# Equal-length matmuls in a row, and a model clock that holds traced matmul durations

## The chip, the core and the metric

The kernel runs on one core of a Trainium2 chip. The metric is the device time of one execution in microseconds; of the kernel before there are three runs. Engines are called by the profile's names: PE multiplies matrices, PEld is its weight loading, DVE, ACT and POOL are the vector, scalar and general engines, SP issues DMAs.

## The reference

Two layers act on one sequence of 256 tokens with 1024 features, all in float32. A layer is a feed-forward block, a mixer and a second feed-forward block:

```python
x = x + 0.5 * swiglu_ffn(rms_norm(x, ffn1_norm[l]), ffn1_w_gate_up[l], ffn1_w_down[l])
h = rms_norm(x, mix_norm[l])
rg_x, rg_g, sb_q, sb_k, sb_v, c_q, c_kv, k_r, gate_logits = jnp.split(h @ w_in[l], split_points, axis=-1)
...
merged = g_a * (y_a @ w_branch_a[l]) + g_b * (y_b @ w_branch_b[l]) + g_c * (y_c @ w_branch_c[l])
x = x + merged @ w_out[l]
x = x + 0.5 * swiglu_ffn(rms_norm(x, ffn2_norm[l]), ffn2_w_gate_up[l], ffn2_w_down[l])
```

The feed-forward blocks are 1024 to 2 x 2816 and 2816 to 1024. The mixer has three branches: a gated linear recurrence (`y_a`), an attention with stick-breaking weights over 8 heads (`y_b`), and an attention with low-rank queries and keys (`y_c`). A final normalisation ends it.

## The kernel before, in words

Activations are kept with the features on the partitions and the 256 tokens along the row. Every float32 value that enters a large product is split into a high part in the type float32r and the rest, also in float32r, and a product is made of three of the four part products: high by high, high by low, low by high.

The weights stream from HBM in units of 1 MB (the tile `raw`). A piece of 128 x 1024 of a unit is split by one copy on ACT (tile `hi`) and one subtraction on DVE (tile `lo`); three `raw`, four `hi` and four `lo` buffers rotate. The split activations lie in the tiles `r`, where the high and the low part of the same 128 features stand beside each other, 256 columns each.

Most products are made by `feature_group` (line 511). A group makes 2 x 128 output features for 256 tokens in two PSUM banks (tile `acc`, or two tiles `side`); the index `b` is the bank. For each 128 input features (one entry of `kts`) and each bank it issues two matmuls: one with the high weights as stationary operand and 512 moving columns, the activations' high and low part side by side (a hi matmul), and one with the low weights and only the 256 columns of the high part (a lo matmul), which adds to the first half of the same bank. `held` holds one entry of `kts` at a time, so one round of the loop is four matmuls. Only the closing entries of a group with `last` are collected to four. `token_group` and `narrow_group` make other layouts with matmuls of one length: 512, 256 or 320 columns.

A feed-forward block runs 22 groups of 8 entries for gate and up, and four groups of 22 entries for down (the last block has two token groups in their place). A mixer runs some 60 groups in the order of the table `MIX_ORDER` (line 31). Between them stands the side work: attention scores, cumulative sums, the recurrence's gates, transposes, normalisations. These are Python generators whose instructions are queued and put between the groups' matmuls by a planner (`Tasks`, line 222). After each round of a group `tick` looks at the front of every queue, and `fits` (line 266) asks a model clock whether the instruction may go: a side matmul goes if its inputs are ready at most 60 ns after the model's PE time, within a budget `SIDE` of 350 ns a round; an instruction on ACT or DVE goes if it starts soon after the model's PE time, and if it is not urgent it must also end within `LIMIT`, 1800 ns of it. `drain` puts in a task without asking, when a group needs its result. The model clock adds up costs per engine; the cost of an instruction is set in `Op.__init__` (line 180 for PE), and `emit` (line 195) also puts in an ACT table load where an activation needs a function that the loaded table does not hold. All engines run their instructions in the order in which they were put in.

All of this goes through one helper, so most rows of the profile bear line 201.

Of the kernel before, what the change touches and what calls it, by code (L numbers as in the profile page):

```python
# [6 lines left out]
F32 = mybir.dt.float32  # L7
F32R = mybir.dt.float32r
# [85 lines left out]
class Slots:  # L94


    def __init__(self, tiles):
        self.free = deque(tiles)
# [61 lines left out]
class Op:  # L160


    def __init__(self, engine, name, op, args, kw):
        self.f, self.e, self.args, self.kw = getattr(engine, op), name, args, kw
        self.engine = engine
        out = kw.get("out", args[0] if args else None)
        n = 1
        for d in out.shape[1:]:
            n *= d
        outs = [out] + ([kw["accum_out"]] if kw.get("accum_out") is not None else [])  # L170
        aps = [x for x in (*args, *kw.values()) if hasattr(x, "tensor")]
        self.outs = {x.tensor.name for x in outs}
        self.ins = {x.tensor.name for x in aps if all(x is not o for o in outs)}
        self.table, self.tail = None, 80
        if op == "dma_start":
            self.cost, self.tail = 50, 2500
        elif name == "pe":
            self.tail = 165
            wide = op == "matmul" and args[2].dtype == F32
            self.cost = 2.5 + 0.4167 * (4 * n if wide else max(n, 256))  # L180
        elif name == "act":
            self.table = TABLES.get(kw.get("func"))
            extra = sum(90 for k in ("scale", "bias") if not isinstance(kw.get(k, 0.0), (int, float)))
            self.cost = 95 + extra + 0.833 * n
        elif name == "dve":
            fast = op in ("tensor_scalar", "tensor_copy") and all(x.space != bass.MemoryType.PSUM for x in aps)
            rate = {"reciprocal": 6.5, "tensor_tensor_scan": 2.1}.get(op, 0.55 if fast else 1.042)
            self.cost = 68 + rate * n
        else:
            self.cost = 150 + (166 if kw.get("op") == ALU.pow else 2.1) * n  # L190

    def when(self, c, after=0.0):
        return c.start(self.e, self.ins, self.outs, after)
# [144 lines left out]
def trunk(tc, xT_in, pos_in, w_in, rgw_in, fin_in, const_in, out):  # L338
# [4 lines left out]
    with ctx:  # L343
# [86 lines left out]
        def next_sub():  # L430
            i = st["sub"]
            st["sub"] += 1
            split_to(i // 2 + AHEAD)
            h, lo = piece_t[i // 2]
            piece_t.pop(i // 2 - 1, None)
            c = slice((i % 2) * 512, (i % 2 + 1) * 512)
            return h[:, c], lo[:, c]
# [44 lines left out]
        def bank():  # L482
            while not acc.free:
                tasks.drain(pend[0], done=lambda: acc.free)
                if pend[0]["done"]:
                    pend.popleft()
            return acc.now()

        def small_banks():
            tasks.wait(lambda: len(side.free) >= NT)  # L490
            return [side.now() for _ in range(NT)]

        def finish(evac, a, early=None):
            t = tasks.spawn(evac(a), urgent=True, early=early)
            if type(a) is not list:
                pend.append(t)
            return t

        def bank_of(a, b):
            return a[b] if type(a) is list else a[:, b]  # L500
# [10 lines left out]
        def feature_group(kts, evac, last=0):  # L511


            nk = len(kts)
            a = small_banks() if last or nk <= 2 else bank()
            held = []
            for i, (h, _, hl) in enumerate(kts):
                if i % 2 == 0:
                    wh, wl = next_sub()
                held.append((i, h, hl, wh, wl))  # L520
                if nk - last <= i < nk - 1:
                    continue
                for b in range(2):
                    for j, h, hl, vh, vl in held:
                        c = slice((j % 2) * 256 + b * 128, (j % 2) * 256 + (b + 1) * 128)
                        pe.matmul(bank_of(a, b), vh[:, c], hl, start=j == 0, stop=False, skip_group_check=True)
                        pe.matmul(bank_of(a, b)[:, 0:256], vl[:, c], h, start=False, stop=j == nk - 1, skip_group_check=True)
                held = []
                tasks.tick()
            return finish(evac, a, tasks.LAST if last else None)  # L530
# [223 lines left out]
        def ffn(nm, ntasks, nxt, final=False, extra=None, xg=None):  # L754
# [24 lines left out]
            for c in range(KF):  # L779
                if xg and c < PLAIN:  # L780
                    ht[c] = plain_group(c, xg, gen_h(c), (ntasks, nm))
                    if c == 0:
                        split_to(2 * PLAIN + 1, 0)
                    if c == PLAIN - 1:
                        FT.give(*xg)
                else:
                    ht[c] = feature_group(kts, gen_h(c))
                if c == 6 and extra:
                    tasks.spawn(extra())
                if c == 3 and final:  # L790
                    xk = {}
                    tokens = tasks.spawn(tokens_of_x(xk))
# [16 lines left out]
            for n in () if final else range(4):  # L809
                out_tasks.append(feature_group(Hidden(), lambda a, n=n: update_x(n, a, 0.5, nxt), last=4 if n == 3 else 0))  # L810
                if n == 0:
                    FT.give(nm["rb tile"])
# [541 lines left out]
        for p in range(4):  # L1354
            for h in range(2 if p == 0 else 1):
                c = slice(h * 256, (h + 1) * 256) if p == 0 else slice(0, 512)
# [160 lines left out]
```

## Time and profile before

| | us |
|---|---|
| median of three runs (lowest, highest) | 1463.38 (1461.54, 1464.88) |
| the profiled execution's own time | 1464.41 |
| its span, first to last instruction | 1462.6 |
| PE busy | 1446.7 (99%) |
| DVE busy | 1110.9 (76%) |
| ACT busy | 889.7 (61%) |
| granted clock of PE, mean | 0.999 |

A matmul's row gives its start and how long it was in the pipeline; matmuls overlap there, so the time that one costs is read from the distance between starts, or from the number of matmuls in a window, and not from its own duration.

### The profile page before, as it was taken

The page shows a single profiled execution, that of the slowest core. Times are in us where ns is not written, and L with a number is a line of the kernel's source. Part 1 is how long each engine was busy: PE and PEld are TensorE (multiplying, and loading weights), DVE is VectorE, ACT ScalarE, POOL GpSimd, SP SyncE. Part 2 cuts the span into 40 slices and gives each one's busy share as a digit, 9 for nine tenths or more (in the row PEclk, how much of TensorE's full clock was granted, in tenths as well). Part 3 has the DMA queues.
Part 4 walks back from the last instruction along what each step waited for, and adds up shares of the span by engine and source line. Part 5 has one row for each costly group of instructions (what it writes and reads, how often), then busy time and mean ns, then how long its engine had stood idle before and what let it go on. Part 6 is the DMA issues. An engine that isn't in the chain of part 4 may idle for free.

```text
span 1462.6 us, 20835 instructions
## 1 busy us (share of the span) xinstructions
PE 1446.7 (99%) x8276; PEld 1264.1 (86%) x8276; DVE 1110.9 (76%) x1548; ACT 889.7 (61%) x1365; POOL 142.5 (10%) x118
## 2 busy tenths in 40 slices
PE   9999999999999999999999999999999999999998
PEld 8888889888888888888888888898888888888886
DVE  6887567689987788876677776676989877877853
ACT  4665446888665556565455554478885656566643
POOL 2000001123410000000000000111324000100001
PEclk9999999999999999999999999999999999999999
DMA  7554554444543455455545455544445434555552
GB/s 264 180 201 179 197 180 167 165 151 147 198 145 145 171 182 195 178 197 190 188 175 195 177 197 178 196 166 147 149 166 180 173 123 170 198 187 199 178 200 87
DMA packets 37507, 258.17 MB, mean 177 GB/s; under 512 B 4257, under 2 KB 4641, under 8 KB 6817
## 3 DMA queue, kind: packets, MB, share of 16 engines
q1 hardware_dynamic: 35856, 253.16, 48.0%
q0 software_dynamic: 832, 2.62, 0.6%
q8 instruction: 65, 1.06, 0.3%
q10 hardware_dynamic: 720, 1.05, 0.2%
q14 instruction: 34, 0.27, 0.1%
HBM read 255.77 MB, written 1.05 MB: 176 GB/s over the span
## 4 chain that ended last, share of the span: by engine, by line
PE 91%; DVE 6%; issue 1%; DMA 1%; ACT 1%; POOL 0%; ACTq 0%; POOLq 0%; DVEq 0%
PE acc L201 76%; PE side L201 15%; DVE lo L201 3%; DVE f L201 2%; DVE r L201 1%; DMA raw<-w 1%; ACT hi L201 0%; DMA x<-xT 0%; ACT f L201 0%; POOL rms L201 0%; ACT r L201 0%; ACTq L396 0%; POOLq L1513 0%; DVE rms L201 0%; DVEq L201 0%
## 5 line engine op out<-in xcount | busy, mean ns | idle before, releaser
L201 PE MATMUL acc<-r,hi 128*128 128x512 f32 x3116 | 1121.4, 402 | 0.0
L201 PE MATMUL acc<-r,lo 128*128 128x256 f32 x3116 | 871.5, 280 | 0.0
L201 DVE TENSOR_TENSOR lo<-raw,hi 128x1024 fp32r<-128x1024 f32 (+1 forms) x478 | 591.2, 1239 | 236.2 <-ACT hi L201 235.1
L201 PEld LDWEIGHTS acc<-r,hi 128*128 128x128 f32 x3116 | 584.9, 188 | 131.4
L201 PEld LDWEIGHTS acc<-r,lo 128*128 128x128 f32 x3116 | 588.1, 189 | 2.5
L201 ACT CAST hi<-raw 128x1024 fp32r<-128x1024 f32 (+1 forms) x478 | 497.0, 1045 | 134.8 <-PE acc L201 94.7
L201 POOL TENSOR_TENSOR f<-f,f 128x512 f32<-128x512 f32 (+1 forms) x51 | 89.5, 1761 | 1047.7 <-ACT f L201 963.9
L201 ACT COPY f<-acc 128x512 f32<-128x512 f32 x164 | 96.2, 586 | 124.3 <-PE acc L201 120.4
L201 ACT ACTIVATE f<-f 128x256 f32<-128x256 f32 (+3 forms) x190 | 94.9, 502 | 84.6 <-DVE f L201 83.4
L201 DVE TENSOR_TENSOR f<-acc,f 128x512 f32<-128x512 f32 x166 | 113.8, 686 | 39.9 <-ACT f L201 39.3
L201 DVE TENSOR_TENSOR f<-f,f 128x512 f32<-128x512 f32 (+1 forms) x177 | 125.0, 706 | 7.9 <-ACT f L201 1.6
L201 PE MATMUL acc<-hi,r 128*128 128x512 f32 (+2 forms) x344 | 96.8, 358 | 0.0
L201 ACT CAST r<-f 128x256 fp32r<-128x256 f32 (+2 forms) x130 | 58.5, 455 | 60.8 <-DVE f L201 59.8
L201 PE MATMUL side<-r,hi 128*128 128x512 f32 x260 | 92.3, 396 | 0.0
L201 PE MATMUL side<-r,lo 128*128 128x256 f32 x260 | 72.7, 280 | 0.0
L201 PE MATMUL side<-f,f 128*128 128x256 f32 (+1 forms) x320 | 71.5, 327 | 0.0
L201 PEld LDWEIGHTS acc<-hi,r 128*128 128x128 f32 x344 | 61.6, 189 | 8.4
L201 DVE TENSOR_TENSOR r<-f,r 128x256 fp32r<-128x256 f32 (+2 forms) x130 | 64.7, 502 | 1.9 <-ACT r L201 1.9
L201 PE MATMUL acc<-lo,r 128*128 128x512 f32 (+2 forms) x172 | 61.1, 355 | 0.0
L201 PEld LDWEIGHTS side<-r,hi 128*128 128x128 f32 x260 | 48.8, 188 | 11.3
L201 PEld LDWEIGHTS side<-f,f 128*128 128x128 f32 x320 | 45.8, 190 | 4.8
L201 PEld LDWEIGHTS side<-r,lo 128*128 128x128 f32 x260 | 49.0, 189 | 0.0
(95 smaller groups left out, 841.4 us busy)
## 6 DMA issues: line engine op xcount, KB each, us to landing
raw<-w SPq DMA_DIRECT2D x239, 1024.0 KB, 4.8
f<-rgw POOLq DMA_DIRECT2D x8, 256.0 KB, 3.3
raw<-w SPq DMA_DIRECT2D x4, 256.0 KB, 5.4
out<-f SPq DMA_DIRECT2D x4, 256.0 KB, 2.2
x<-xT ACTq DMA_DIRECT2D x3, 256.0 KB, 5.8
f<-fin POOLq DMA_DIRECT2D x2, 256.0 KB, 3.7
cst<-const SPq DMA_DIRECT2D x1, 336.0 KB, 7.7
x<-xT ACTq DMA_DIRECT2D x2, 128.0 KB, 4.0
```

Of the source, the lines that this page charges most:

```text
L201: return self.f(*self.args, **self.kw)
```

## The change

The loop of `feature_group` now issues the hi matmuls of both banks first and then the lo matmuls of both banks. Where `last` is set, each bank is still finished by itself, its hi matmuls first and then its lo matmuls. The model cost of a matmul on PE is given by a new function; the lengths, types and number of matmuls do not change.

```diff
             self.tail = 165
-            wide = op == "matmul" and args[2].dtype == F32
-            self.cost = 2.5 + 0.4167 * (4 * n if wide else max(n, 256))
+            self.cost = self.streamed(op, args[2].dtype if op == "matmul" else F32, n)
...
+    @staticmethod
+    def streamed(op, dtype, n):
+
+        if op == "transpose":
+            return max(109, 0.852 * n)
+        if dtype == F32:
+            return 2 * max(112, 0.852 * n)
+        if dtype == F32R:
+            return 13.5 + 0.4167 * max(n, 256)
+        return 30 + 0.4167 * n
...
-                for b in range(2):
-                    for j, h, hl, vh, vl in held:
-                        c = slice((j % 2) * 256 + b * 128, (j % 2) * 256 + (b + 1) * 128)
+                for bs in ((0,), (1,)) if last else ((0, 1),):
+                    work = [(b, j, h, hl, vh, vl, slice((j % 2) * 256 + b * 128, (j % 2) * 256 + (b + 1) * 128)) for b in bs for j, h, hl, vh, vl in held]
+                    for b, j, h, hl, vh, vl, c in work:
                         pe.matmul(bank_of(a, b), vh[:, c], hl, start=j == 0, stop=False, skip_group_check=True)
+                    for b, j, h, hl, vh, vl, c in work:
                         pe.matmul(bank_of(a, b)[:, 0:256], vl[:, c], h, start=False, stop=j == nk - 1, skip_group_check=True)
```

For a hi matmul of 512 columns the model cost goes from 215.9 to 226.9 ns, for a lo matmul of 256 columns from 109.2 to 120.2 ns.

The first place is PE in the gate and up groups of the first feed-forward block, three entries of `kts`; `acc_84` is a group's pair of banks, `r_90` and `r_91` are split activations. Before:

```order
L201 MATMUL acc_84<-r_90,hi 128x512
L201 MATMUL acc_84<-r_90,lo 128x256
L201 MATMUL acc_84<-r_90,hi 128x512
L201 MATMUL acc_84<-r_90,lo 128x256
L201 MATMUL acc_84<-r_90,hi 128x512
L201 MATMUL acc_84<-r_90,lo 128x256
L201 MATMUL acc_84<-r_90,hi 128x512
L201 MATMUL acc_84<-r_90,lo 128x256
L201 MATMUL acc_84<-r_91,hi 128x512
L201 MATMUL acc_84<-r_91,lo 128x256
L201 MATMUL acc_84<-r_91,hi 128x512
L201 MATMUL acc_84<-r_91,lo 128x256
```

The same twelve matmuls now:

```order
L211 MATMUL acc_84<-r_90,hi 128x512 x2
L211 MATMUL acc_84<-r_90,lo 128x256 x2
L211 MATMUL acc_84<-r_90,hi 128x512 x2
L211 MATMUL acc_84<-r_90,lo 128x256 x2
L211 MATMUL acc_84<-r_91,hi 128x512 x2
L211 MATMUL acc_84<-r_91,lo 128x256 x2
```

The lengths change every two matmuls and no longer at every one. In the seven groups with `last` (the last down group of three feed-forward blocks, and two groups of each mixer) the entries before the closing four keep the order of before, since one entry and one bank make a single hi and a single lo matmul; the closing four entries make runs of four.

The second place is ACT in the first layer's mixer, in the groups `rgg1` and `rgg2`; `f_112<-f_112 128x384` before and `f_136<-f_136 128x384` now is stick-breaking work, `f_118<-side_88,cst` now is a gate of the recurrence, `f_113` and `f_109` are gates. Before, twelve rows hold one table load:

```order
L136 ACT_TABLE_LOAD
L201 ACTIVATE f_109<-f_109 128x512
L201 CAST hi<-raw 128x1024
L201 ACTIVATE f_113<-f_110 128x512
L201 CAST hi<-raw 128x1024
L201 COPY f_123<-acc_84 128x512
L201 ACTIVATE f_141<-side_87 128x384
L201 CAST r_103<-f_121 128x512
L201 ACTIVATE f_112<-side_89 128x384
L201 ACTIVATE f_113<-f_113 128x512
L201 CAST hi<-raw 128x1024
L201 ACTIVATE f_136<-f_123 128x512
```

Now, a little earlier in the same mixer, three stand in twelve rows:

```order
L136 ACT_TABLE_LOAD
L211 ACTIVATE f_118<-side_88,cst 128x256
L211 ACTIVATE f_119<-side_88,cst 128x256
L211 ACTIVATE f_136<-side_86 128x384
L136 ACT_TABLE_LOAD
L211 ACTIVATE f_136<-f_136 128x384
L211 CAST hi<-raw 128x1024
L211 COPY f_137<-acc_84 128x512
L211 ACTIVATE f_136<-f_136 128x384
L136 ACT_TABLE_LOAD
L211 ACTIVATE f_121<-f_118,tiny,s_77 128x256
L211 CAST hi<-raw 128x1024
```

Recurrence and stick-breaking work now alternate on ACT, and each change of function loads a table. Over the whole kernel the order holds 33 table loads before and 45 now, the twelve more in the two mixers.

The third place is PE where the recurrence's last gates are computed, in the first layer's mixer; `side_86<-r_98,r_97` are those gates' products. Before, they stand in the groups `rgg3` and `gb0`:

```order
L201 MATMUL side_87<-f_112,f_119 128x128
L201 MATMUL side_86<-r_98,r_97 128x256 x2
L201 MATMUL acc_85<-r_92,hi 128x512
L201 MATMUL acc_85<-r_92,lo 128x256
L201 MATMUL acc_85<-r_92,hi 128x512
L201 MATMUL acc_85<-r_92,lo 128x256
L201 MATMUL side_86<-r_98,r_97 128x256 x4
L201 MATMUL acc_85<-r_92,hi 128x512
L201 MATMUL acc_85<-r_92,lo 128x256
L201 MATMUL acc_85<-r_92,hi 128x512
L201 MATMUL acc_85<-r_92,lo 128x256
L201 MATMUL side_88<-r_93,r_103 128x256 x4
```

Now the last of them stand some twenty matmul rounds later, in the group `gb2`:

```order
L211 MATMUL side_86<-r_93,r_104 128x256 x2
L211 MATMUL acc_84<-r_105,hi 128x512 x2
L211 MATMUL acc_84<-r_105,lo 128x256 x2
L211 MATMUL side_86<-r_93,r_104 128x256 x3
L211 MATMUL acc_84<-r_90,hi 128x512 x2
L211 MATMUL acc_84<-r_90,lo 128x256 x2
L211 MATMUL side_86<-r_93,r_104 128x256
```

Two pairs of the recurrence were fed together before (`r_98` and `r_93` in turn); now one pair is fed at a time, with rounds of the group between its matmuls.

## Rows read from the trace of the kernel before

**Rows 1.** The page: its first line, and part 1, engines.

```profile
span 1462.6 us, 20835 instructions
PE 1446.7 (99%) x8276; PEld 1264.1 (86%) x8276; DVE 1110.9 (76%) x1548; ACT 889.7 (61%) x1365; POOL 142.5 (10%) x118
```

**Rows 2.** Waits of PE: who waits for whom, us in total, times, longest.

```profile
PE side L201 <- DVE r L201: 4.7, 4, 1.5
PE side L201 <- DVE f L201: 2.0, 2, 1.1
```

**Rows 3.** Groups by form, whole span: count | busy us, mean ns | idle before.

```profile
L201 PE MATMUL acc<-r,hi 128*128 128x512 f32 x3116 | 1121.4, 402 | 0.0
...
L201 PE MATMUL side<-r,hi 128*128 128x512 f32 x260 | 92.3, 396 | 0.0
```

**Rows 4.** The same view, 30 to 190 us (first layer, first feed-forward block).

```profile
L201 PE MATMUL acc<-r,hi 128*128 128x512 f32 x433 | 153.0, 399 | 0.0
...
L201 PE MATMUL side<-r,hi 128*128 128x512 f32 x21 | 7.5, 399 | 0.0
```

**Rows 5.** The same view, 560 to 730 us (first layer, second feed-forward block).

```profile
L201 PE MATMUL acc<-r,hi 128*128 128x512 f32 x455 | 157.8, 391 | 0.0
...
L201 PE MATMUL side<-r,hi 128*128 128x512 f32 x37 | 12.9, 391 | 0.0
```

**Rows 6.** The same view, 750 to 910 us (second layer, first feed-forward block).

```profile
L201 PE MATMUL acc<-r,hi 128*128 128x512 f32 x439 | 155.2, 399 | 0.0
...
L201 PE MATMUL side<-r,hi 128*128 128x512 f32 x15 | 5.3, 399 | 0.0
```

**Rows 7.** The same view, 1300 to 1390 us (second layer, second block).

```profile
L201 PE MATMUL acc<-r,hi 128*128 128x512 f32 x261 | 90.5, 391 | 0.0
```

**Rows 8.** Timeline of PE, token group, 512 columns throughout: start, us, what, count.

```profile
1400.30 0.61 PE L201 MATMUL acc<-hi,r 128*128 128x512 f32 x2
1400.75 0.39 PE L201 MATMUL acc<-lo,r 128*128 128x512 f32 x1
1400.98 0.61 PE L201 MATMUL acc<-hi,r 128*128 128x512 f32 x2
```

**Rows 9.** Timeline of PE, narrow group, 256 columns throughout.

```profile
246.99 0.40 PE L201 MATMUL acc<-hi,r 128*128 128x256 f32 x2
247.23 0.28 PE L201 MATMUL acc<-lo,r 128*128 128x256 f32 x1
247.35 0.40 PE L201 MATMUL acc<-hi,r 128*128 128x256 f32 x2
```

**Rows 10.** Timeline of PE, a token group with four short side matmuls in it.

```profile
286.41 0.64 PE L201 MATMUL side<-r,r 128*128 128x256 f32 x4
286.88 0.40 PE L201 MATMUL acc<-hi,r 128*128 128x512 f32 x1
287.12 0.40 PE L201 MATMUL acc<-lo,r 128*128 128x512 f32 x1
287.35 0.62 PE L201 MATMUL acc<-hi,r 128*128 128x512 f32 x2
287.81 0.39 PE L201 MATMUL acc<-lo,r 128*128 128x512 f32 x1
288.04 0.61 PE L201 MATMUL acc<-hi,r 128*128 128x512 f32 x2
288.50 0.39 PE L201 MATMUL acc<-lo,r 128*128 128x512 f32 x1
```

**Rows 11.** Groups on ACT: the table loads.

```profile
L136 ACT ACT_TABLE_LOAD x33 | 42.3, 1283 | 5.4 <-DMA x<-xT 4.8
```

**Rows 12.** Windows in the first mixer: us, then each engine's busy time, clock.

```profile
225.00:330.00 105.00, 105.00 (x631) 93.11 (x630) 81.02 (x111) 86.06 (x133) 21.02 (x20) 1.00 0.44 158
350.00:500.00 150.00, 148.94 (x876) 130.43 (x875) 125.40 (x201) 95.92 (x171) 20.83 (x16) 1.00 0.45 161
```

**Rows 13.** Timeline of PE in the first mixer: one wait of a recurrence gate.

```profile
340.09 0.63 PE L201 MATMUL side<-r,r 128*128 128x256 f32 x3 [1.45 <-DVE r L201]
```

## The prediction

> **What bounds the kernel now.** I read the page's busy times first, then PE's waits, then PE's groups in four windows, then single stretches of PE's timeline. PE is busy 1446.7 of 1462.6 us [rows 1], and it stands waiting for little: 4.7 us for split operands of the recurrence and 2.0 us for other operands of side work [rows 2]. In the windows looked at, its granted clock is 1.00, the 2.4 GHz level [rows 12]. So the end is set by how fast PE gets through its queue of matmuls, and the change touches the order of the most frequent ones: 3116 + 260 = 3376 hi matmuls, each with one lo matmul, so 3376 pairs [rows 3].
>
> Busy time does not say what a pair costs, because matmuls overlap in the pipeline. I count pairs in windows that hold nothing else. From 30 to 190 us there are 433 + 21 = 454 hi matmuls [rows 4]; one is cut by the edges, so a pair takes 160 / 453 = 353.2 ns. From 750 to 910 us there are 439 + 15 = 454 again, 353.2 ns [rows 6]. From 560 to 730 us there are 455 + 37 = 492, and 170 / 491 = 346.2 ns [rows 5]; from 1300 to 1390 us 261, and 90 / 260 = 346.2 ns [rows 7]. The same instructions in the same order run at two paces, and the mean time in the pipeline tells them apart at a glance: 399 ns at the slow pace, 391 at the fast one.
>
> What would matmuls of one length cost? Three of 512 columns start within 1400.98 - 1400.30 = 0.68 us, so one takes 226.7 ns [rows 8]. Three of 256 take 247.35 - 246.99 = 0.36 us, 120 ns each [rows 9]. Together 346.7 ns: that is the fast pace. So alternating lengths cost nothing in two of the four feed-forward blocks, and about 6.6 ns a pair in the other two.
>
> **The change part by part.** *Order of the pairs.* It removes no matmul. What it can remove is the 6.6 ns, where they are paid. The slow blocks hold 20 x 16 + 4 x 44 = 496 pairs (two groups of the first block use other matmuls) and 22 x 16 + 4 x 44 = 528, together 1024, which at 6.6 ns is 6.8 us. The fast blocks hold 528 and, without its token groups, 352: 880 pairs with nothing to gain. The remaining 3376 - 1024 - 880 = 1472 pairs stand in the mixers, where side matmuls break the stream again and again; no window there holds pairs alone, so I take half of the price as an estimate, 1472 x 3.3 = 4.9 us. Together 11.7 us. Of the 3376 pairs, 140 keep the order of before: the entries ahead of the closing four in three last down groups (18 x 2 each) and in four last groups of the mixers (4 x 2 each). At stake: 11.7 x 3236 / 3376 = 11.2 us, 0.8% of the span.
>
> How much of it goes? The order before changes length at every matmul, twice in each pair. The new order changes twice in each round of two pairs; with the 56 pairs of the closing entries set aside there are 3180 / 2 = 1590 rounds. If the loss belongs to the changes of length, each costing on average what it costs now, half of it goes: 5.6 us. The bounds are nothing lost (gain 11.2 us) and a price per change that grows with the length of the run before it. For the second bound there is one stretch: four 256s and then only 512s. From 286.41 to 288.50 us stand four 256s and seven 512s, which at the even rates would take 4 x 120 + 7 x 226.7 = 2067 ns; they take 2090 [rows 10]. So one settled change back and forth costs about 23 ns, and the long starts come after the change, not at it: 240, 230, then 460 for two, 230, 460 for two. The first two 512s alone, with the 256s ahead, run from 286.41 to 287.35, 940 ns against 933: 7 ns. A round in the new order is just that short: two 512s after two 256s. At 7 ns a round the total is 1590 x 7 = 11.1 us, what is paid now; at 23 ns it is 36.6 us, 25 us more than now. The nearest rows for short runs are those of the alternation itself, and they hold both zero and 6.6 ns a pair, so I take the half, a gain of 5.6 us.
>
> The evacuation of a group is not moved by this: its last matmul is still the lo matmul of the second bank. A lo operand is wanted one hi matmul later than before, the second bank's hi weights one lo matmul earlier (120 ns), and they lie in the same piece as the first bank's. DVE and ACT split pieces ahead, and no wait of PE for `hi` or `lo` is in the list [rows 2].
>
> The Trainium skill ("TensorE: Matmul & The Clock Gate", section "LDWEIGHTS (loading the stationary operand)") puts a weight load at its columns over 1.2 GHz, some 107 ns for 128 columns. By that a 256-column matmul, which streams for as long, would just cover the next load, and two short ones in a row would have no slack, which speaks against this change. The trace does not bear it out as a stall: 256s in a row hold 120 ns, with the same 13.3 ns over their streaming time as the 512s.
>
> *The model clock.* A pair's cost in the model rises from 325 to 347 ns, so the planner's PE time runs about 7% faster against ACT and DVE than it did. Side instructions are put at other places in the mixers. Two things follow. First, twelve more table loads at 1283 ns each [rows 11], 15.4 us of ACT, six loads a mixer. From 225 to 330 us ACT was busy 86.06 of 105 us and DVE 81.02 [rows 12]; five more loads bring ACT there to some 92. It still fits, so the cover is ACT's idle time. If that cover failed, each load would delay the next `hi` behind it on ACT, then `lo` on DVE and then PE: at most 15.4 us, at least nothing; and below nothing by the waits that go. I take 2 us, near the end at nothing, because PE shows no wait for `hi` or `lo` at 82% ACT. Second, the waits of 4.7 and 2.0 us [rows 2] stand where the planner put a side matmul before its input; an example is the 1.45 us at 340.09 [rows 13]. Their places move: the last gates of the recurrence now come in the group `gb2`, one pair at a time. They could all go (6.7 us less) or double, because the old cost, lower than the traced one, left each side matmul about 7% more room than the model knew, and that room is gone. I take them as they are, at zero change.
>
> *The sum.* 1462.6 - 5.6 + 2 = 1459.0 us of span. The profiled execution took 1464.41, 1.8 us more than its span, and lay 1.0 us above the median of the three runs, 1463.38. So 1459.0 + 1.8 - 1.0 = 1459.8 us.
>
> **The rivals.** *The order is indifferent.* The loss stays where it is, because it hangs on something that the order of two matmuls does not touch. For it: the same order had both paces for some 170 us each, so the order alone does not decide. Against: runs of one length show no loss at all [rows 8, 9]. Time: 1463.4 + 2 = 1465.4, and without the 2 us of table loads 1463.4.
>
> *All of the loss goes.* Rounds of two and two run at the even rate everywhere, as the alternation does in two blocks. For it: both lengths settle at an even rate. Against: the long starts after the change in rows 10. Time: 1463.4 - 11.2 = 1452.2 without the 2 us for table loads, 1454.2 with them.
>
> *Slower: each round pays for settling.* After a run of 256s several 512s start late [rows 10]. Before, the queue could lock into a beat in which the change was free; in rounds of two no such beat may exist, and each round would pay between the 7 ns of its first two 512s and the 23 ns of the settled change. At the middle, 15 ns, it is 1590 x 15 = 23.9 us, 12.7 more than now: 1476.1. It decides from (11.2 + 2.9) / 1590 = 8.9 ns a round on. For it speaks the only stretch with a run of several 256s ahead of a run of 512s; against it that a round of two is far from settled.
>
> *Slower: the mixers wait.* The room of 7% is gone and six more loads stand in each mixer: the waits of 6.7 us double and the loads cost 5 us, 11.7 in all, while the pairs bring 5.6: 1469.5. For it: ACT at 82% and DVE at 84% of the two windows [rows 12]. Against: PE waits for few operands now.
>
> **How the numbers follow.** Half of the loss goes, 0.34, with 1456 to 1463 as its own range; all of it goes, 0.14; indifferent, 0.20; settling, 0.18; mixers wait, 0.14. About 0.2%, 2.9 us, is what a measurement of this kernel can tell from no change. Faster by more: most of the forecast's case (0.26) and all of the second (0.14), with a little of the indifferent one if some waits go (0.02): 0.42. Slower by more: the two slower cases but for a tenth, and some of the indifferent one: 0.33. Within: 0.25. The range runs from 1451, a little under all of the loss gone, to 1475, just under the middle price of settling; a tenth is left out above and a little below.
>
> **What would show it.** Right: in 30 to 190 us some 460 hi matmuls and a mean time in the pipeline nearer 391 than 399; two starts of 512s about 227 to 233 ns apart, then two of 256s about 118; PE's waits in the mixers of the same size as before; 45 table loads, and no wait of PE for `hi` or `lo`. Wrong: fewer pairs than 454 in that window (settling), fewer than 492 from 560 to 730 us, where nothing can be gained but something lost, or a new row of PE waits in the mixers. If the feed-forward blocks again show two paces, the order does not decide the beat.

## The result and the profile after

The changed kernel takes 1481.49 us (median of four runs, 1480.93 to 1483.88), the kernel before 1463.86 in the same comparison. The ratio is 1.0128, 95% interval 1.0113 to 1.0142: slower by 17.6 us, and above the predicted range. The profiled execution of the changed kernel took 1483.88 us with a span of 1482.0.

The first line of its page and the engines; they answer to [rows 1]:

```profile
span 1482.0 us, 20830 instructions
PE 1454.4 (98%) x8276; PEld 1265.5 (85%) x8276; DVE 1106.9 (75%) x1548; ACT 901.0 (61%) x1377; POOL 135.7 (9%) x118
```

PE runs the same 8276 matmuls. Its busy time grew by 7.7 us and the time in which it was not busy by 11.7; the two are the 19.4 us of span.

The pairs first, since they were the larger part of the prediction. The groups by form in three windows that hold pairs alone (30 to 190, 575 to 735 and 765 to 925 us) answer to [rows 4 to 6]; the columns are count | busy us, mean ns:

```profile
L211 PE MATMUL acc<-r,hi 128*128 128x512 f32 x439 | 137.9, 395 | 0.0
...
L211 PE MATMUL side<-r,hi 128*128 128x512 f32 x21 | 7.5, 399 | 0.0
...
L211 PE MATMUL acc<-r,hi 128*128 128x512 f32 x441 | 138.6, 395 | 0.0
...
L211 PE MATMUL side<-r,hi 128*128 128x512 f32 x19 | 6.6, 394 | 0.0
...
L211 PE MATMUL acc<-r,hi 128*128 128x512 f32 x428 | 134.4, 395 | 0.0
...
L211 PE MATMUL side<-r,hi 128*128 128x512 f32 x33 | 11.5, 394 | 0.0
```

460, 460 and 461 hi matmuls stand in 160 us each: 348.6, 348.6 and 347.8 ns a pair. The two paces of before, 353.2 and 346.2, have become one between them. The timeline of PE shows a round of it (start us, us in the pipeline, what, count):

```profile
99.85 0.62 PE L211 MATMUL acc<-r,hi 128*128 128x512 f32 x2
100.31 0.40 PE L211 MATMUL acc<-r,lo 128*128 128x256 f32 x2
100.54 0.63 PE L211 MATMUL acc<-r,hi 128*128 128x512 f32 x2
```

Two 512s take 0.46 us, two 256s 0.23; a round is 0.69 to 0.70.

So the pairs gained, and the loss lies elsewhere. The waits of PE answer to [rows 2] (who waits for whom: us in total, times, longest):

```profile
PE side L211 <- DVE f L211: 6.2, 4, 1.6
PE side L211 <- DVE r L211: 4.9, 6, 1.4
PE acc L211 <- DVE f L211: 3.1, 3, 2.7
PE acc L211 <- DVE lo L211: 2.1, 4, 0.7
PE side L211 <- ACT f L211: 2.0, 4, 0.5
```

The 2.7 stands at 10 us, before the first mixer; a wait of this kind at the start comes and goes from trace to trace (order_only, below, has none, half_lo has one of 2.9). The rest, 15.6 us, lies in the mixers, where 6.7 us stood before. Some are new in kind: main matmuls now wait for `lo`.

The table loads, and the two windows of [rows 12]:

```profile
L136 ACT ACT_TABLE_LOAD x45 | 57.7, 1283 | 5.3 <-DMA x<-xT 4.6
```

```profile
225.00:330.00 105.00, 103.19 (x612) 90.41 (x611) 78.81 (x106) 86.82 (x132) 21.18 (x20) 1.00 0.45 158
...
350.00:500.00 150.00, 143.85 (x825) 125.32 (x824) 121.20 (x201) 92.85 (x169) 22.65 (x17) 0.98 0.42 152
```

The last line has a granted clock of 0.98 where it was 1.00. Where that comes from is seen on PE's timeline in the first mixer, with the wait ahead of a matmul in brackets:

```profile
352.16 0.34 PE L211 MATMUL side<-r,tri_r 128*128 128x384 f32 x1
353.94 0.44 PE L211 MATMUL side<-r,tri_r 128*128 128x384 f32 x1 [1.44 <-DVE r L211]
...
355.38 0.80 PE L211 MATMUL side<-r,hi 128*128 128x512 f32 x1 [0.54 <-ACT f L211]
355.97 0.63 PE L211 MATMUL side<-r,lo 128*128 128x256 f32 x2
356.39 1.05 PE L211 MATMUL side<-f,f 128*128 128x256 f32 x2
356.89 1.41 PE L211 MATMUL side<-r,hi 128*128 128x512 f32 x2
```

and in the windows of the same stretch (the granted clock is the third number from the end):

```profile
354.00:356.00 2.00, 1.46 (x6) 1.05 (x7) 2.00 (x4) 1.49 (x3) 1.04 (x1) 0.85 0.85 356
356.00:358.00 2.00, 2.00 (x7) 1.72 (x6) 2.00 (x3) 0.63 (x1) 1.15 (x1) 0.50 0.26 107
358.00:360.00 2.00, 2.00 (x11) 1.76 (x11) 1.97 (x4) 0.94 (x2) 0.00 (x0) 0.80 0.00 0
```

PE waits 1.44 and then 0.54 us, and the clock falls to 0.50, the 1.2 GHz level. What is missing from 1.00 in the three lines is (0.15 + 0.50 + 0.20) x 2 = 1.7 us of full speed. This happens four times in the mixers of the changed kernel (near 356, 404, 1087 and 1135 us), 6.8 us in all, and not once in the kernel before. That is what the clock withheld, and so the most that it can have cost; part of it can fall where PE would have had to wait anyway. Of the four runs of clock_only, a kernel with the same new costs that is introduced below, one had a mean granted clock of 0.999 and took 1481.37 us, another 0.995 and 1481.29 us.

The account of the 19.4 us, by the distances between PE's matmuls: pairs -3.8 us (what they take above the even rate fell from 9.5 to 5.7); the start +2.3, which varies by run and is no part of the change; the two mixers +20.9, of which waits of PE some 9 and the low clock at most 6.8; the remaining 5 us and more are not traced to a row.

### The profile page after: what moved, and what is told of

Same layout as the page of the kernel before. It is cut to its first block, busy times and chain, and to the rows that moved or that the text cites. A ratio compares the mean times of both kernels' runs of the same rounds, so it can differ in the third digit from the quotient of the medians.

```text
span 1482.0 us, 20830 instructions
## 1 busy us (share of the span) xinstructions
PE 1454.4 (98%) x8276; PEld 1265.5 (85%) x8276; DVE 1106.9 (75%) x1548; ACT 901.0 (61%) x1377; POOL 135.7 (9%) x118
## 4 chain that ended last, share of the span: by engine, by line
PE 79%; ACT 9%; DVE 7%; issue 3%; POOL 1%; DMA 0%; ACTq 0%; POOLq 0%; DVEq 0%
PE acc L211 67%; PE side L211 13%; ACT f L211 4%; DVE lo L211 4%; DVE f L211 3%; ACT L136 3%; ACT hi L211 2%; POOL f L211 1%; DMA x<-xT 0%; DVE r L211 0%; ACT r L211 0%; POOL rc L211 0%; ACTq L406 0%; POOLq L1524 0%; POOL rms L211 0%
## 5 line engine op out<-in xcount | busy, mean ns | idle before, releaser
L211 PE MATMUL acc<-r,hi 128*128 128x512 f32 x3116 | 1000.0, 402 | 0.4 <-DVE f L211 0.4
L211 PE MATMUL acc<-r,lo 128*128 128x256 f32 x3116 | 614.8, 279 | 2.1 <-DVE lo L211 2.1
L211 PEld LDWEIGHTS acc<-r,hi 128*128 128x128 f32 x3116 | 482.3, 189 | 5.4 <-DVE f L211 0.8
L211 POOL TENSOR_TENSOR f<-f,f 128x512 f32<-128x512 f32 (+1 forms) x51 | 81.0, 1589 | 1074.4 <-ACT f L211 967.8
L211 PE MATMUL acc<-hi,r 128*128 128x512 f32 (+2 forms) x344 | 100.0, 363 | 0.0
L211 PE MATMUL side<-r,hi 128*128 128x512 f32 x260 | 87.9, 408 | 1.1 <-ACT f L211 1.1
L211 PE MATMUL side<-r,lo 128*128 128x256 f32 x260 | 61.4, 283 | 0.0
```

Source lines behind the costliest of these rows:

```text
L211: return self.f(*self.args, **self.kw)
```

## The experiments

All kernels below are set against the kernel before on the same chip. "Old costs" is the old cost line, "new loop" the new order of hi and lo matmuls; the loads are the table loads that ACT runs. The kernel before itself had a median of 1461.9 to 1465.3 us in these comparisons, so a difference between medians of two comparisons is good to some 2 us; where that matters, the ratios are used.

| kernel | median us | ratio to before, 95% interval | loads |
|---|---|---|---|
| order_only | 1461.38 | 0.9990 (0.9980 to 1.0001) | 33 |
| clock_only | 1480.81 | 1.0120 (1.0101 to 1.0139) | 45 |
| loads12 | 1469.36 | 1.0046 (1.0028 to 1.0064) | 45 |
| others_up | 1467.37 | 1.0030 (1.0019 to 1.0040) | 43 |
| rest_only | 1486.10 | 1.0141 (1.0113 to 1.0169) | 33 |
| f32r_only | 1473.00 | 1.0057 (1.0039 to 1.0075) | 39 |
| room200 | 1477.58 | 1.0085 (1.0067 to 1.0104) | 37 |
| calm12 | 1473.99 | 1.0062 (1.0045 to 1.0080) | 25 |
| no_loads | 1467.71 | 1.0027 (1.0015 to 1.0038) | 1 |
| order_no_loads | 1460.75 | 0.9986 (0.9977 to 0.9995) | 1 |
| half_lo | 1467.42 | 1.0028 (1.0012 to 1.0044) | 45 |
| order_half_lo | 1452.20 | 0.9925 (0.9908 to 0.9941) | 33 |
| no_loads_half_lo | 1455.18 | 0.9947 (0.9933 to 0.9960) | 1 |
| shift_05 | 1468.19 | 1.0037 (1.0024 to 1.0049) | 33 |
| shift_10 | 1467.14 | 1.0030 (1.0020 to 1.0041) | 39 |
| light | 1460.34 | 0.9985 (0.9976 to 0.9994) | 33 |

### One half of the change at a time

order_only is the changed kernel with the old cost line, clock_only the changed kernel with the old loop:

```diff
-            self.cost = self.streamed(op, args[2].dtype if op == "matmul" else F32, n)
+            self.cost = 2.5 + 0.4167 * (4 * n if op == "matmul" and args[2].dtype == F32 else max(n, 256))
```

> The new order of the matmuls in a round, with the old model costs; side work stands where it stood before. If the two parts of the change add up, pairs gain what the changed kernel's profile shows (348.4 ns a pair everywhere, against 353.2 and 346.2): 9.5 us of loss above the even rate fall to about 5.7, so 3.8 us faster, 1459 to 1461. If the order itself made PE wait for lo or hi operands, it is slower than 1464.

> The old order of the matmuls in a round, with the new model costs. If the planner's new order of side work is the whole loss, it takes 1463.9 + 17.6 + 3.8, about 1485, with waits of PE in the mixers as in the changed kernel and the two paces of the pairs back. If the loss needs both parts, it lies well below 1480.

The new loop alone is worth 3.8 us of span (1458.8 against 1462.6) and about 1 us of the median, which the interval does not tell from nothing: the profiled execution of the kernel before, 1464.41 us, is one of its longer ones (1460.70 to 1466.91 in these 19 runs). The new costs alone lose 18.5 us against the before of that comparison, 1462.34, as much as the whole change, if 4 us less than the 1485 that I expected. The model costs enter nothing but the planner's choices, so the loss is the planner's new order.

The two paces did not come back as I had them. In clock_only, which has the old loop, the second layer's first block (765 to 925 us) runs at the fast pace, 160 / 462 = 346.3 ns, and the first layer's at the slow one:

```profile
L211 PE MATMUL acc<-r,hi 128*128 128x512 f32 x425 | 147.4, 391 | 0.0
...
L211 PE MATMUL side<-r,hi 128*128 128x512 f32 x38 | 13.2, 391 | 0.0
```

So the pace is not a property of a block, and what the slow blocks paid in one profiled execution need not be there in another.

### Are the twelve more loads the price?

loads12 is order_only with twelve extra loads of another table, each just ahead of one that is there:

```diff
+            c.loads = getattr(c, "loads", 0) + 1
+            if c.loads % 15 in (3, 4, 5, 6, 7, 8):
+                self.engine.preload_act_table_set("gelu_and_others")
             c.load(self.engine, self.table[0])
```

> The new order of matmuls with the old model costs, and twelve more ACT table loads of 1283 ns, six in each mixer, each right before one that was there; the planner does not know of them. Theory A (side matmuls put in with no room are the loss): the loads mostly fit into idle time of ACT, 0 to 5 us slower than the new order alone. Theory B (table loads are the loss): 12 to 20 us slower than the new order alone, since each delays hi, then lo, then PE.

Twelve loads cost 8.0 us over order_only, 0.67 us each: more than the 2 us predicted, less than half of the loss, and between the two ranges that I had given. And rest_only below has 33 loads and the longest median of all; calm12 has 25 and is some 10 us slower than order_only. The number of loads does not order these times. Their place differs too: the extra loads of loads12 stand at 237 to 278 us in the first mixer, while from 300 to 345 us the changed kernel has ten loads where the kernel before has two, at 325.90 and 336.69.

### Is it the ratio of the engines, or a part of the cost table?

In the expectations of this section and the one above, Theory A is that side matmuls have lost their room, Theory B that the loads are the loss. others_up multiplies the model's costs of ACT, DVE and POOL by 1.068, so that their ratio to PE is about the old one. rest_only keeps the old cost for float32r and takes the new one for all else; f32r_only the reverse. room200 asks for 200 ns more between an operand and its matmul; calm12 lets a side task change the table no sooner than twelve rounds after the last change.

```diff
-            self.cost = 95 + extra + 0.833 * n
+            self.cost = 1.068 * (95 + extra + 0.833 * n)
...
-            return 13.5 + 0.4167 * max(n, 256)
+            return 2.5 + 0.4167 * max(n, 256)
...
-                s = max(s, w[0] + self.CROSS)
+                s = max(s, w[0] + cross)     # cross = self.CROSS + (200 if e == "pe" else 0)
...
+        if op.table and op.kw["func"] not in c.funcs and self.step < c.since + 12:
+            return False
```

> The changed kernel with the model costs of ACT, DVE and POOL also raised by 6.8%, the ratio by which a pair's cost rose. Theory A (room): the ratio of before is back, side matmuls get room again, PE's waits in the mixers fall from 23 us towards 8 and the time to 1459 to 1468. Theory B (table loads): the planner's order still holds 43 loads, so it stays at 1475 to 1482.

> The changed kernel with the old model cost for float32r matmuls (the pairs) and the new ones for float32, bfloat16 and transposes; the planner's order holds 33 table loads. If the pairs' cost is what spoiled the plan, this is about the new order alone, 1459 to 1465. If the small matmuls' costs did it, about 1480.

> The changed kernel with the new model cost for float32r matmuls alone; 39 table loads. If the pairs' cost is what spoiled the plan: 1472 to 1482. By the theory that loads are the loss (8 us for twelve, from the run with twelve blind loads) six more make 1465 with nothing else.

> The changed kernel, and the model lets PE start 200 ns later after the end of what it reads than before (330 instead of 130 ns between engines, for PE alone). 37 table loads. Theory A (no room): PE's waits for DVE and ACT in the mixers fall below 10 us and the time lies at 1460 to 1468. Theory B (loads): four more loads than before cost 3 us, 1464, the same; then the waits tell: by A they fall for every kind of operand, by B only where a load stands ahead.

> The changed kernel, with the new model costs and no more room, and a planner that lets an activation change ACT's table only twelve rounds after the last change (unless a group needs it). 25 table loads, eight fewer than before and twenty fewer than in the changed kernel. Theory A (no room): side matmuls still have no room, so 1470 to 1480. Theory B (loads): twenty loads less at 0.67 us each give back 13 us, 1465 to 1470; if loads are all of it, 1455 to 1462.

Against order_only, by the ratios, some 6 us of loss remain with the engines' ratio restored, 14 of 20 with more room for the operands. The two parts of the table do not add: the part for float32r, which holds the 7%, loses 10 us, the rest alone 22, both together 20, the last two not told apart by their intervals. others_up came out where the theory of room had it, with 43 loads. room200, made to test that theory, did not: it lies 10 us above the range, and 17.6 us of waits of PE for DVE and ACT remain in its mixers, where I had said below 10. calm12 lies in the range for room and above the one for loads, f32r_only at the low end of the one for the pairs' cost, and rest_only above both of its own. PE's waits in rest_only:

```profile
PE side L211 <- DVE r L211: 7.9, 4, 2.9
PE side L211 <- DVE f L211: 7.7, 4, 2.5
PE acc L211 <- DVE f L211: 4.5, 4, 2.5
PE side L211 <- ACT r L211: 2.5, 2, 1.2
```

The same kind of wait, in other places, more often and longer: ten waits of side matmuls with 1.8 us on average, where the kernel before has six with 1.1, and no load more than before. room200 speaks against missing room as the cause; what is left to look at is why DVE's results come late. That rest_only loses by the same chain as the changed kernel is not shown: neither of the edits below was made on it.

### What DVE is late for

The stretch to look at is the middle of a mixer. From 311 to 436 us the windows of before and of after (PE, PEld, DVE, ACT, POOL busy, clock), first before:

```profile
311.00:436.00 125.00, 121.60 (x711) 106.53 (x711) 115.23 (x162) 89.56 (x149) 38.81 (x29) 1.00 0.45 162
```

```profile
311.00:436.00 125.00, 117.97 (x661) 101.97 (x660) 105.34 (x143) 91.85 (x143) 34.08 (x27) 0.97 0.45 159
```

Before, DVE is busy 92% of this stretch; it has hardly any time to lose. After, it got through 143 instructions instead of 162, and its own waits say why, before and after in the same stretch:

```profile
DVE lo L201 <- ACT hi L201: 7.4, 9, 2.0
```

```profile
DVE lo L211 <- ACT hi L211: 16.4, 12, 3.0
```

ACT's timeline of the changed kernel just ahead of it:

```profile
311.40 1.28 ACT L136 ACT_TABLE_LOAD   x1
312.70 0.47 ACT L211 ACTIVATE f<-side,cst 128x256 f32<-128x256 f32 x1
313.07 1.04 ACT L211 CAST hi<-raw 128x1024 fp32r<-128x1024 f32 x1
314.01 0.58 ACT L211 COPY f<-acc 128x512 f32<-128x512 f32 x1
314.48 0.53 ACT L211 CAST r<-f 128x384 fp32r<-128x384 f32 x1
314.90 0.50 ACT L211 ACTIVATE f<-side 128x384 f32<-128x384 f32 x1
315.42 1.28 ACT L136 ACT_TABLE_LOAD   x1
316.71 0.53 ACT L211 ACTIVATE f<-f 128x384 f32<-128x384 f32 x1
317.14 1.03 ACT L211 CAST hi<-raw 128x1024 fp32r<-128x1024 f32 x1
318.08 0.52 ACT L211 ACTIVATE f<-f 128x384 f32<-128x384 f32 x1
318.61 1.28 ACT L136 ACT_TABLE_LOAD   x1
```

ACT works without a pause, nearly half of the time on loads (3 x 1.28 of 8.5 us), and each `hi` here comes one activation behind a load. DVE waits for it; as I read it, what DVE loses there it cannot make up in a stretch that needs 92% of it, and PE pays at 353 to 412 us.

From here on there are three theories, under new letters. A: the loads alone are the price. B: ACT and DVE form one chain in the middle of a mixer, and it has become longer than PE's work beside it. C: the new places of the side matmuls make PE wait, whatever the supply. Two edits test them, each on the changed kernel and on order_only, with the order of instructions held. In no_loads one table is loaded and all functions are computed as a sigmoid. In half_lo DVE subtracts half of each piece in the mixers (all but those of `ckv`), while the model charges the whole; the second half of the low weights is left out.

```diff
-        engine.preload_act_table_set(table)
+        if not self.funcs:
+            engine.preload_act_table_set("sigmoid_and_others")
...
+        kw = dict(self.kw, func=AF.Sigmoid) if self.table else self.kw
```

```diff
+                    if st.get("mix") and not kinds_of[2 * i].startswith("ckv"):
+                        o.args = (lo[:, 0:512], src[:, 0:512], h[:, 0:512].bitcast(F32))
```

> The changed kernel with its order of instructions kept, but only one table load: the model still charges 1283 ns for each of the 45, the loads are not issued, and every exponential, logarithm, tanh and silu is computed as a sigmoid instead, which has the one table. Theory A, the loads of the new plan are its price: the mixers' loss falls from some 16.7 us each to that of the same edit on the kernel with the old costs, within 2 us of it, and the time to about 1460. Theory B, ACT and DVE in the middle of a mixer form one chain that has become longer than the matmuls beside it, and loads are only a part of its length: between the two, 1463 to 1472, and PE's waits for f, r and lo stay in kind. Theory C, the new places of the side matmuls make PE wait whatever the supply is: no more than the 0.67 us a load that twelve extra loads have cost, 1481 - 45 x 0.3 = 1468 or more.

> The control: the same edit (one table load, all functions as sigmoid) on the kernel with the new loop and the old costs, which has 33 loads. All theories: its mixers lose 6.3 us each now; without loads they lose 3 to 6, so 1453 to 1460. If it gains as much as the changed kernel does, loads cost both the same and don't make the difference.

> The changed kernel with its order kept, but in the mixers DVE subtracts only the first half of each piece's low part (128x512 instead of 128x1024; both halves of the piece then use it), while the model charges the full one. DVE has some 0.55 us less to do for each of the mixers' pieces. Theory A (loads on ACT): DVE is not the limit, PE's waits stay, 1476 to 1481. Theory B (one chain of ACT and DVE): the chain shortens, the mixers' loss falls from 16.7 us to 10 or less each, 1460 to 1468. Theory C (places in PE's queue alone): 1478 to 1481.

> The control: the same half subtraction in the mixers of the kernel with the new loop and the old costs. Theory B: its mixers' loss of 6.3 us falls too, by 1 to 4 us each, 1453 to 1460, since the same chain bounds it, only less. Theories A and C: no change, 1460 to 1462.

Without loads the changed kernel gains 13.8 us, order_only 0.6, which its intervals do not tell from nothing. With half the low parts the changed kernel gains 14.1, order_only 9.2, more than Theory B had allowed it; order_no_loads lies just above the range that all three had given. (By the ratios each of the larger gains is 0.3 to 1.0 us higher.) So a load costs 0.31 us on average in the new order and next to nothing in the old one: there ACT's idle time hides it, here the load lies on the chain. And DVE's work costs time in both.

The controls say how much of the difference is whose. The changed kernel lies 20.1 us above order_only; with both kernels without loads it is 7.0, with both at half the low parts 15.2. The loads at their new places are thus the larger part, some 13 of the 20 us. But Theory A had called for 2 us or less where 7.0 are left.

The chain of waits from 300 to 440 us shows both. Before:

```profile
by line: PE acc L201 43.3%; PE side L201 21.9%; DVE lo L201 13.0%; DVE f L201 10.5%; DVE r L201 4.2%; issue 3.9%; ACT hi L201 1.8%; ACT f L201 1.2%; ACT r L201 0.3%; DVEq L201 0.0%; ACTq L201 0.0%
```

After:

```profile
by line: DVE lo L211 15.7%; PE acc L211 15.4%; ACT f L211 12.1%; issue 11.9%; DVE f L211 10.4%; ACT L136 10.1%; PE side L211 9.3%; ACT hi L211 8.3%; POOL f L211 3.1%; DVE r L211 1.5%; ACT r L211 1.3%; POOL rc L211 0.8%; DVEq L211 0.1%; POOL
```

order_half_lo:

```profile
by line: PE acc L211 74.7%; PE side L211 25.5%; issue 0.0%
```

Before, PE's share of the chain there is 65%, and DVE has 28%. After, PE has 25%, ACT with its loads over 30%. With half the low parts and the old order, PE has all of it. The chain tells more here than the sum of DVE's waits for `hi`, 16.4 us above: no_loads_half_lo, below, has 16.5 us of them from 311 to 436 us and hardly any loss, for DVE is busy only 93.55 of the 125 us there.

### Do the two together carry everything?

> The changed kernel with its order kept and both earlier edits together: one table load only (every function as a sigmoid) and in the mixers half of each piece's low part on DVE. Theory B (one chain of ACT and DVE carries the loss): PE's waits in the mixers go, as they went with half the low parts in the kernel with the old costs, and the time falls to 1453 to 1458. Theory C (the places of the side matmuls): it stays at 1463 or more, since each edit alone gave 1467.5 and their gains overlap.

Both edits in one kernel give 1455.18, a gain of 26.3 us; alone they gave 13.8 and 14.1, so they nearly add, where Theory C had them overlap. It lies 3.0 us above order_half_lo, of the 20.1 us between the kernels without the edits. The places of PE's side matmuls by themselves can account for about that much: Theory C is left with some 3 us. (order_only with both edits was not run; without its loads alone it gained 0.6 us.) Theory B carries the loss, with the loads as the larger member of the chain, and Theory A, that they alone are the price, leaves 7.0 us unexplained.

### Does the size of the cost change matter?

shift_05 and shift_10 are order_only with 3.0 and 3.5 for the constant 2.5:

```diff
-            self.cost = 2.5 + 0.4167 * (4 * n if op == "matmul" and args[2].dtype == F32 else max(n, 256))
+            self.cost = 3.0 + 0.4167 * (4 * n if op == "matmul" and args[2].dtype == F32 else max(n, 256))
```

> The new loop with the old cost line, but 3.0 in place of 2.5 ns as its constant: PE's matmuls cost 0.5 ns more in the model, 0.2 to 0.5%. The planner's order of PE, DVE and ACT in the mixers still changes in many places; the number of loads stays at 33. If a plan loses by the size and direction of the cost change: 1460 to 1463, as with 2.5. If any new plan loses because the table of groups and the limits were fitted to one plan: 1466 to 1480.

> The same with 3.5 ns, 1.0 ns more than the old constant; 39 loads. By size and direction: 1460 to 1464. By any new plan: 1466 to 1480, and not above shift_05 by more than the loads make (6 at 0.3 to 0.7 us).

Half a nanosecond in the model costs 6.8 us, a whole one 5.8, as the expectation for any new plan had it. The planner asks yes or no at every instruction, and one changed answer moves all that follows. Of the old order and nine others that I ran (the changed kernel, clock_only, the five from others_up to calm12 and these two), the old one is the fastest by 5.8 us at least. That the group order and the limits were fitted to that one order fits this but is not shown: I fitted none of them to the new costs.

### A version that follows

light is order_only with 66 small DVE instructions, each a product with one number per row, run on ACT in the same places; every value is still computed.

```diff
+        if moved:
+            self.f, self.args, self.kw = moved.engine.activation, (), {"out": args[0], "in_": args[1], "func": AF.Copy, "scale": args[2]}
...
-                    dve.tensor_scalar(f, bank_of(a, t), scales[t], None, op0=ALU.mult)
+                    dve.tensor_scalar(f, bank_of(a, t), scales[t], None, op0=ALU.mult, moved=act)
```

> The new loop with the old costs, and in the mixers' order as it is, the products with one number per row that DVE makes (evacuations by a scale, the attention weights' division, the diagonals for the norms, the second half of the latents; about 13 us of DVE in each mixer) run on ACT, at the same places of the program and with the model still charging DVE. Theory B: DVE's work in the middle of the mixers holds 9 us of the kernel with the old costs, as half the low parts showed; these take away some 5 us of it in each middle: 1455 to 1459. Theories A and C: 1460 to 1462, or slower if ACT's new work delays the splitting.

It is faster than the kernel before, by 0.15% (0.06 to 0.24), and 21 us faster than the changed one, but at most 1 us below order_only, which the intervals do not tell from nothing: it missed the range of Theory B and lies in that of A and C. Less was moved out of the dense stretch than I had counted on: from 311 to 436 us DVE is busy 113.44 us, in order_only 115.51, so 2.1 us went and not 5. Its waits of PE show what is left:

```profile
PE side L214 <- DVE r L214: 4.7, 4, 1.5
...
PE acc L214 <- DVE f L214: 0.4, 2, 0.2
PE side L214 <- ACT f L214: 0.4, 2, 0.2
```

The 2.5 us of waits for `f` that order_only has are nearly gone; the 4.7 us for `r`, of [rows 2], stand at 335 to 339 us, ahead of most of the moved work.

## Why the prediction was wrong, step by step

*The order of the pairs* was right in kind. Half of the price was taken to go, 5.6 us; 3.8 went in the profiled executions, about 1 us of the median. The 6.8 us for the slow blocks were read from one execution and taken as fixed; clock_only ran one of the two blocks at the fast pace in the old order. That half would go was a choice between two bounds. The slow blocks gained 4.6 ns a pair, but the fast ones lost 2.4, since a round of two pairs has a price of its own: 0.69 to 0.70 us against 2 x 346.7 = 693 ns. The settling rival put at least 7 ns on a round; the windows show 2 x 348.6 - 693.4 = 3.8.

*The model clock* is the step that failed: "I take 2 us, near the end at nothing", and for the waits "I take them as they are, at zero change". Against 2 us stand 20.9 us of the profiled span. The bounds that I had worked out, 15.4 us for the loads and 6.7 for waits that double, add to 22.1, so the sum lay inside them, though PE's waits alone grew by 8.9 us and passed their bound; I chose the low end, and the range did not reach the high one. Three readings led there.

First, the cover. "It still fits, so the cover is ACT's idle time" rested on windows of 105 and 150 us [rows 12], where DVE shows 77 and 84%. The stretch that lies across both, 311 to 436 us, has DVE at 92%. The sum of busy times fits in both; but an engine that works in order loses what it waits, and at 92% there is little room to get it back.

Second, "PE waits for few operands now" was read as room. It was the end of a chain that already ran through DVE for 28% of that stretch, and order_half_lo shows 9 us waiting there in the old order. The chain of waits in a window of the mixer would have told it; I read PE's waits alone.

Third, the loads were priced one by one, beside idle time, while the new order put ten of them into 45 us, from 300 to 345 us, in the rows above three to five instructions apart, with a `hi` behind each.

*The rival in which the mixers wait* had the mechanism, with 1469.5 us. Its price was 11.7 us; 20.9 came. Up to 6.8 us of that is the low clock, of which none of the cases knew. Its chance, 0.14, was the lowest given, with one other's.

*What would show it*: "a new row of PE waits in the mixers" was named as a sign of wrong, and it is there, and so is the wait for `lo` that was not to come. Another sign of wrong came too: from 560 to 730 us, where 492 hi matmuls stood, 170 us at the new pace hold 488, a loss of the fast blocks. The 460 hi matmuls and the 45 loads came as said; the mean time in the pipeline, 395 ns, lies halfway between 391 and 399.

## What to carry to other kernels

A planner that asks yes or no at each instruction turns a truer number in its model into a new order of everything behind it; price such a change by the spread between orders (here 6 to 22 us, even for 0.5 ns), not by what the number itself is worth, and keep the old order until a new one has been timed. Before costing work on another engine at nothing, cut the windows to the stretch where that engine is densest and read the chain of waits there: few waits of PE can be the end of a chain with nothing to spare. Test such a chain by making each member shorter with the order held, on both kernels, and read the difference between the kernels: here the two edits took off 14 us each and 26 together, but of the 20 us between the kernels the one without loads took 13 and the one on DVE 5.

## What the runs showed of the hardware that was not expected

Short waits can bring the clock down. After 1.44 and 0.54 us of waiting within 3 us the granted clock was 0.50 for some 3 us, 1.7 us of full speed. The kernel before has a wait of 1.45 us at 340.09 [rows 13] and one of 0.89 us at 336.3, and its granted clock from 336 to 344 us is 1.00. All four falls in the changed kernel's mixers stand behind two waits that follow each other closely; no_loads_half_lo and light have none in theirs. Two close waits are neither needed nor enough: in no_loads the clock is 0.50 from 402 to 404 us behind a single wait of 3.09 us at 401.26, and in clock_only it stays at 1.00 from 400 to 408 us, with waits of 0.65 us at 400.69 and 1.27 at 402.80. What decides it stays open. The Trainium skill ("TensorE: Matmul & The Clock Gate", section "What's actually happening") says of this clock that "the default state is throttled, and activity releases the throttle"; the fall to 0.50 behind the waits agrees.

A table load takes ACT 1.28 us and no more: the load at 315.42 starts 20 ns after the activation ahead of it ends (314.90 + 0.50), and the next activation starts at 316.71. The Trainium skill ("ScalarE: Activation LUTs", section "What ACT_TABLE_LOAD costs") adds a drain of about 1380 ns to each switch; no such pause stands in these rows.

One DVE instruction of the same shape takes 0.69 or 1.77 us. From the timelines of DVE and of POOL in the changed kernel:

```profile
323.53 0.69 DVE L211 TENSOR_TENSOR f<-f,f 128x512 f32<-128x512 f32 x1
...
327.13 1.77 DVE L211 TENSOR_TENSOR f<-f,f 128x512 f32<-128x512 f32 x1
```

```profile
327.06 1.29 POOL L211 TENSOR_TENSOR f<-f,f 128x512 f32<-128x512 f32 x1
```

The long one runs beside a tensor-by-tensor instruction of POOL. In the whole trace, 155 DVE instructions of this form run with none of POOL's beside them, and all take 0.69 to 0.70 us; 14 overlap a tensor-by-tensor instruction of POOL, and they take 0.69 to 1.78 us, eight of them over 1 us. That POOL's work lengthens DVE's was not tried by itself; if it does, taking POOL's products out of the middle of the mixers would shorten the same chain.
